# A two-layer hybrid mixer block in fp32 on one core: loads and residual sums of the downward MLP issued step by step, and the second layer's modulation computed in its own input projection

## The chip, the cores and the metric

The kernel runs on one core of one Trainium2 chip. The metric is the device time of one execution in microseconds, as the median of several runs. All data is fp32; a product is made of three matmuls of an fp32r high part and an fp32r rest (high x high, high x rest, rest x high).

## What is computed

Two layers (`DEPTH = 2`) over 1024 image tokens and 256 context tokens with 1024 channels. Each layer normalizes, modulates with a shift and a scale computed from a condition vector, projects into the columns of three mixers (an RWKV-7 scan, a gated delta net and a Fourier mixer), projects back, and ends with an MLP. Cut to what matters here:

```python
for l in range(DEPTH):
    last = l == DEPTH - 1
    m = (jax.nn.silu(c) @ w_mod[l] + b_mod[l]).reshape(b, N_MOD, 1, D_MODEL)
    mc = (jax.nn.silu(c_ctx) @ w_mod[l] + b_mod[l]).reshape(N_MOD, D_MODEL)
    uc = modulate(rmsnorm(xc, norm1_g[l]), mc[0], mc[1]) @ w_in[l]
    ux = modulate(rmsnorm(xl, norm1_g[l]), m[:, 0], m[:, 1]) @ w_in[l]
    ...                                   # the three mixers give yx (and yc)
    xl = xl + m[:, 2] * (yx @ w_out[l])
    hx = modulate(rmsnorm(xl, norm2_g[l]), m[:, 3], m[:, 4])
    xl = xl + m[:, 5] * sq_relu_mlp(hx, mlp_w1[l], mlp_w2[l])
    if not last:
        ...                               # the same for the context xc, with mc
return rmsnorm(xl, final_g)
```

The context is not carried behind the second layer, so that layer needs the modulation of columns 16 to 47 (in blocks of 128; shift and scale of the second norm, and the gates) for the image alone, one vector, where the first layer needs two.

## The kernel before, in words

`layer(l)` runs input projection, mixers and MLP one after the other; `run` calls it twice and then `final`. Tokens stand in pieces: A and B are 512 image tokens each, C is the context. In program order the stages are:

- **Input projection** (`layer`, from L2238). RWKV columns, gates z, Fourier columns, then 12 jobs of the delta net's convolution: a projection on PE, on DVE four multiply-adds and a scaling over up to 1282 columns (`gy`, `gu`), norms, and transposes on PE. Weights are 128 x 1024 blocks that `wsplit` (L281) loads as two raw tiles, copies to the high part on ACT and subtracts to the rest on POOL. The generator `mod` (L2242) is advanced at fixed places (L2249, L2250, L2269, L2270).
- **Modulation** (`mod_part`, L444). Twelve groups of four column blocks are made of eight loads of 256 KB each (tile `wmod`). The first of the eight is scaled on ACT into `macc`, each further one is a multiply-add on DVE (L462); for a second vector ACT scales and POOL adds (L464, L465). PE sums over the partitions (L474). In the first layer all groups from 16 on are made in the input projection; the second layer's twelve groups are made in the first layer's MLP (L1947).
- **Mixers** (`mixers`, L2034), whose end makes the output projections, the norms and the start of the MLP. From L2195 on it splits the weights of `early` blocks ahead.
- **MLP up** (`up`, L1613). One step of Strassen's scheme (Winograd's form) for the halves A and B of the tokens: 16 pairs of blocks with seven products of 12 matmuls each (`prod`, L1682), whose factors for the tokens are the tiles T1 to T4 and B22 (`norm_sums`, L559) and for the weights the tiles uS and uA (`up_parts`, L1567). While the sums for B are not ready, `ahead(n)` (L1642) makes the first `early` pairs' upper-left block from two plain products; such a pair later skips A11 and A12 and reads the result back (L1729). The squared activations and their sums go to DRAM as `h`.
- **Context down** (`context_down`, L1779, first layer only): 32 parts of 24 matmuls with 256 columns. Its caller (L1956) advances it and, from part 9 on, the first part of the downward pass.
- **MLP down** (`halves_down`, L1826): two halves f of the hidden blocks, seven products p in the order of `DOWN` (L39), eight steps n each. A step splits one `h` tile (loaded as `hraw`, five steps ahead) into `hu` on ACT and DVE (L1854, L1855) and one weight tile into `wu` on ACT and POOL (L1857, L1858), forms the next sums of weights in place on DVE (`we`, `wo`, `ws`; L1860 to L1866), and makes 12 matmuls (L1917). `ready(i + 2)` (L1909) is called two steps ahead of the matmuls. At n = 7 the four banks are drained on DVE and the residual `xrA` or `xrB` takes up finished sums (`add`, L1904; L1932 to L1940). The residual is brought back from DRAM by `back_x` (L1512), called at L1964 ahead of all steps; the odd weight tiles are loaded at L1888 to L1891.
- Behind the steps, `mlp` (L1946) makes the squares and sums for the next norm (L1983 to L2001).

Two things set the order of the work around the change. Every engine executes its queue in order, and all loads and stores go through the queue of SP in the order in which they were put there. The framework's scheduler orders independent instructions by the order of the program and by its own estimate of when operands are ready; a tile's place in memory is handed out in program order (`slot`, L163), and who gets it next waits for who had it. The kinds of places are x, w, u and h for tiles and r for raw ones (12 in the MLP, 6 in the input projection).

Of the kernel before, what the change touches and what calls it, by code (L numbers as in the profile page):

```python
# [35 lines left out]
DEC = 0.3032653298563167  # L36

HALVES = ("B11", "B21", "T2", "T3", "T4", "T1", "B22")
DOWN = ("A11", "A12", "S2", "S3", "A22", "S1", "S4")  # L39

COLS = (
# [68 lines left out]
class Net:  # L110
# [1502 lines left out]
    def up(self, l, last, mod, end):  # L1613
# [54 lines left out]
        ahead(1)  # L1668
        sums = self.norm_sums(l, self.kept)
        for n in range(2, 6):  # L1670
            next(sums)
            if n < self.early:
                ahead(n)
        for _ in chain(sums, self.pair):
# [151 lines left out]
    def halves_down(self, l, last):  # L1826
# [18 lines left out]
        def ready(i):  # L1845

            if i >= len(steps):
                return
            f, p, n = steps[i]
            fetch_h(i + 5)  # L1850
            w = {"A11": (even, 0), "A12": (odd, 0), "S2": (even, 0), "S3": (even, 1), "A22": (odd, 1), "S4": (odd, 0)}
            src = sums[n // 2][:, n % 2] if DOWN[p] == "S1" else w[DOWN[p]][0][n][:, w[DOWN[p]][1]]
            u, h, raw = us[i % 3], hs[i % 3], raws.pop(i)
            self.act(h[:, 0], raw)  # L1854
            V.tensor_tensor(h[:, 1], raw, h[:, 0].bitcast(F32), SUB)  # L1855
            self.free(raw)
            self.act(u[:, 0], src)  # L1857
            self.P.tensor_tensor(u[:, 1], src, u[:, 0].bitcast(F32), SUB)  # L1858
            e, o, s1 = even[n], odd[n], sums[n // 2][:, n % 2]
            if p == 0:  # L1860
                V.tensor_tensor(s1, e[:, 1], o[:, 1], ADD)
            elif p == 1:
                V.tensor_tensor(e[:, 0], s1, e[:, 0], SUB)  # L1863
            elif p == 2:
                V.tensor_tensor(e[:, 1], o[:, 1], e[:, 0], SUB)
                V.tensor_tensor(o[:, 0], o[:, 0], e[:, 0], SUB)  # L1866
            for q, ts, o in ((3, even, 0), (6, odd, 1)):
                if p == q:
                    if f == 0:
                        fetch(ts[n], 2 * (n + 8) + o)  # L1870
                    else:
                        self.free(ts[n])
            if p == 5 and f == 1 and n % 2:
                self.free(sums[n // 2])
# [10 lines left out]
                for j in range(5):  # L1885
                    fetch_h(j)
        yield
        for i in range(8):  # L1888
            yield from wait("u")
            odd.append(take("wo", "u"))  # L1890
            fetch(odd[i], 2 * i + 1)  # L1891
        while self.upward:
            yield
        yield "turn"
        for i in range(3):
            us.append(take("wu", "x", F32R))
            hs.append(take("hu", ("x", "x", "w!")[i], F32R))
# [2 lines left out]
        ready(1)  # L1900
        u2, u3 = [take("ms", "x") for _ in range(2)], []
        half = lambda t, b: t[b // 2][:, b % 2]

        def add(pc, b, t):  # L1904
            x = self.block(self.xr[pc], b)
# [2 lines left out]
        for i, (f, p, n) in enumerate(steps):  # L1908
# [6 lines left out]
            for b in range(4):  # L1915
                c = slice(b * 128, b * 128 + 128)
                self.mm3(ps[b], u[:, 0, c], u[:, 1, c], h[:, 0], h[:, 1], n == 0, n == 7)  # L1917
                if n == 7:
# [9 lines left out]
                    else:  # L1928
                        V.tensor_tensor(a, ps[b], a, ADD)  # L1929
                        if nm == "S1":  # L1930
                            V.tensor_tensor(z, ps[b], z, ADD)  # L1931
            for b in range(4) if n == 7 else ():  # L1932
                if nm == "A12":
                    add("A", b, half(u2, b))
                elif nm == "A22":
                    add("A", b + 4, half(u3, b))
                elif nm == "S1":
                    add("B", b + 4, half(u3, b))
                elif nm == "S4":
                    add("B", b, half(u2, b))  # L1940
            if f == 1 and n == 7 and p == 5:
                self.free(*u3)
            yield f, p, n
        self.free(*u2, *us, *hs)

    def mlp(self, l, last):  # L1946
        mod = iter(()) if last else self.mod_part(l + 1, 0, 48, True)  # L1947
        down = self.halves_down(l, last)
        self.upward = True
        if last:  # L1950
# [10 lines left out]
            self.gains(l + 1, 1)  # L1961
        while last and next(down) != "turn":
            pass
        for p in "AB":  # L1964
            self.back_x(f"xm{l}", p)
        sq, sc = [], []
        for f, p, n in down:
            if f == 0 and p == 0 and not last:
                if n == 0:
                    for j in range(2):  # L1970
                        self.squares("C", j, sc)
                elif n == 2:
                    self.rsum("C", sc)
                elif n == 4:
                    norm = self.norms(l + 1, 1, "C")
# [4 lines left out]
                    del self.xr["C"]  # L1980
            if f == 0:
                continue
            if (p, n) == (5, 0):  # L1983
                for j in range(4):
                    self.squares("A", j, sq)
            if (p, n) == (5, 3):
                self.rsum("A", sq)
                sq = []
            if (p, n) == (5, 7) and not last:
                self.first = [self.wsplit(self.win(l + 1, c), kind="w!") for c in (768, 256)]  # L1990
            if (p, n) == (6, 0):
                norm = iter(()) if last else self.norms(l + 1, 1, "A")
                for j in (2, 3):
                    self.squares("B", j, sq, "u")
            if p == 6:
                next(norm, None)
        for _ in norm:
# [36 lines left out]
    def mixers(self, l, last):  # L2034
# [159 lines left out]
        self.outproj(l, "B", yb, lambda b: b % 2 and self.squares("B", b // 2, self.sq))  # L2194
        self.at(1.6)  # L2195
        self.share = "uw"
        self.early = 4
        self.ahead = [self.wsplit(self.w1(l, 2 * n)) for n in range(self.early)]
        self.save_x(f"xm{l}", "B", False)
        self.raw = [self.up_load(l, fb) for fb in range(2)]  # L2200
# [10 lines left out]
    def layer(self, l):  # L2211
# [27 lines left out]
        self.set_rings(d=4, m=4)  # L2239
        self.rwkv_setup(l)  # L2240
        uk = self.rwkv_lora(l)
        mod = iter(()) if l else self.mod_part(l, 16, 48)  # L2242

        def others():

# [64 lines left out]
```

## Time and profile before

| | us |
|---|---|
| median of 3 runs | 4007.14 |
| lowest and highest | 3997.73 and 4032.35 |
| profiled execution, its own time | 4021.84 |
| its span, first to last instruction | 4020.1 |
| mean granted TensorE clock | 0.894 |

In the profiled execution the first layer's input projection runs from about 180 to 620 us, its mixers to 1290, its upward pass to 1776, the context's downward part until 1918 and its downward pass from 1880 to 2247 us. The second layer's input projection ends at about 2690 us, its mixers and output projections at 3325, its upward pass at 3664; its downward pass runs from 3657 to 3996 us, and `final` ends the span.

A line of the profile names engine, line of the kernel, instruction and tiles (written<-read). Most tiles are made by helpers, so that L257 is every matmul, L254 every ACT instruction and L264 every load; the tile tells them apart. A granted clock of 1.00 is TensorE at 2.4 GHz, 0.50 at 1.2 GHz; a value between is the mean of a stretch.

### The profile page before, as it was taken

Reading aid. Unit: us, or ns where it says so; the run is one execution under the profiler, and the core shown is the slowest. Engines: PE = TensorE matmul, PEld = TensorE weight load, DVE = VectorE, ACT = ScalarE, POOL = GpSimd, SP = SyncE. Lnnn points to the kernel's source line nnn. Section 1 sums busy time; section 2 is a strip of 40 time slices with the busy share of each in tenths; the row PEclk is TensorE's granted clock in tenths of the full one; section 3 lists DMA queues with packets and bytes.
Section 4 is the critical chain, followed back from the end, with each engine's and each line's share of the span. In section 5 each row is a group of like instructions: output and inputs, shape, how many; then the busy total and the mean of one; then the engine's idle time right before and its main releaser. Section 6 shows DMA issues by size and latency. Waiting matters only on the chain. (4 is left out here: it accounts for less than half of the span.)

```text
span 4020.1 us, 61983 instructions
## 1 busy us (share of the span) xinstructions
PE 3554.5 (88%) x23262; PEld 2971.3 (74%) x23262; DVE 2776.1 (69%) x4224; ACT 1619.5 (40%) x2947; POOL 1546.8 (38%) x1110
## 2 busy tenths in 40 slices
PE   8998996886888899998999989987698898998998
PEld 5776885775767788888778766876687776887777
DVE  5645777888764776566687744657878667767677
ACT  5433443333344444343434433433343344343443
POOL 1422435332225466434445322114333144554443
PEclk8999887877888999999999999997777898999999
DMA  6333436543466254578643232345344463447432
GB/s 219 107 127 139 122 113 177 150 147 94 132 178 199 88 168 142 169 243 284 194 127 115 67 134 102 105 119 176 98 140 128 149 193 106 158 154 256 157 110 82
DMA packets 546127, 589.83 MB, mean 147 GB/s; under 512 B 37654, under 2 KB 399650, under 8 KB 545826
## 3 DMA queue, kind: packets, MB, share of 16 engines
q1 hardware_dynamic: 545826, 585.86, 46.0%
q8 instruction: 183, 3.00, 0.3%
q14 instruction: 118, 0.97, 0.1%
HBM read 419.62 MB, written 166.10 MB: 146 GB/s over the span
## 5 line engine op out<-in xcount | busy, mean ns | idle before, releaser
L257 PE MATMUL bank<-hu,wu 128*128 128x512 f32 x2688 | 635.6, 398 | 32.5 <-DVE hu L1855 23.7
L294 POOL TENSOR_TENSOR wlo<-wraw,whi 128x512 fp32r<-128x512 f32 x264 | 356.7, 1372 | 777.3 <-ACT whi L254 413.5
L257 PEld LDWEIGHTS bank<-hu,wu 128*128 128x128 f32 x2688 | 514.1, 192 | 151.5 <-DVE hu L1855 32.9
L1855 DVE TENSOR_TENSOR hu<-hraw,hu 128x512 fp32r<-128x512 f32 x224 | 260.5, 1171 | 126.7 <-ACT hu L254 126.6
L1578 POOL TENSOR_TENSOR uS<-us,uS 128x512 fp32r<-128x512 f32 x128 | 193.8, 1528 | 168.7 <-ACT uS L254 155.8
L254 ACT ACTIVATE whi<-wraw 128x512 fp32r<-128x512 f32 (+1 forms) x296 | 178.8, 625 | 196.9 <-DMA wraw<-in_mlp_w_dram 53.0
L465 POOL TENSOR_TENSOR macc<-macc,wmod 128x512 f32<-128x512 f32 x84 | 135.6, 1615 | 188.2 <-ACT wmod L254 185.2
L254 ACT ACTIVATE ms<-ms 128x512 f32<-128x512 f32 x176 | 110.3, 627 | 241.1 <-DVE ms L1631 239.1
L257 PE MATMUL bank<-xhA,whi 128*128 128x512 f32 (+1 forms) x480 | 203.4, 425 | 0.0
L257 PE MATMUL bank<-xlA,whi 128*128 128x512 f32 (+1 forms) x480 | 199.8, 417 | 0.0
L257 PE MATMUL bank<-xhA,wlo 128*128 128x512 f32 (+1 forms) x480 | 197.8, 413 | 0.3 <-POOL wlo L294 0.3
L1858 POOL TENSOR_TENSOR wu<-we,wu 128x512 fp32r<-128x512 f32 x96 | 135.6, 1413 | 161.0 <-ACT wu L254 160.8
L462 DVE SCALAR_TENSOR_TENSOR macc<-wmod,cs,macc 128x512 f32<-128x512 f32 x140 | 135.2, 966 | 85.3 <-DMA wmod<-in_w_mod_dram 43.7
L1858 POOL TENSOR_TENSOR wu<-wo,wu 128x512 fp32r<-128x512 f32 x96 | 131.8, 1374 | 148.3 <-ACT wu L254 146.8
L1578 POOL TENSOR_TENSOR uA<-wraw,uA 128x512 fp32r<-128x512 f32 x96 | 142.5, 1491 | 98.2 <-ACT uA L254 85.8
L712 DVE SCALAR_TENSOR_TENSOR gy<-gu,vt,gy 128x1282 f32<-128x1282 f32 (+1 forms) x96 | 154.6, 1611 | 26.7 <-ACT gy L254 26.0
L1631 DVE TENSOR_TENSOR ms<-bank,ms 128x512 f32<-128x512 f32 x216 | 143.7, 683 | 38.6 <-PE bank L257 20.0
L257 PE MATMUL bank<-xhB,whi 128*128 128x512 f32 (+1 forms) x416 | 165.2, 397 | 5.0 <-ACT ru L254 5.0
L257 PE MATMUL bank<-xlB,whi 128*128 128x512 f32 (+1 forms) x416 | 164.7, 396 | 0.0
L257 PE MATMUL bank<-xhB,wlo 128*128 128x512 f32 (+1 forms) x416 | 164.0, 394 | 0.0
L845 DVE TENSOR_TENSOR iD<-iF,iE 128x31 f32<-128x31 f32 (+15 forms) x310 | 149.7, 484 | 6.5
L846 DVE TENSOR_TENSOR iE<-iE,iD 128x31 f32<-128x31 f32 (+15 forms) x310 | 144.2, 466 | 6.5
(525 smaller groups left out, 9719.6 us busy)
## 6 DMA issues: line engine op xcount, KB each, us to landing
hraw<-h SPq DMA_DIRECT2D x224, 256.0 KB
h<-ms SPq DMA_DIRECT2D x214, 256.0 KB
wraw<-in_mlp_w_dram SPq DMA_DIRECT2D x208, 256.0 KB
wmod<-in_w_mod_dram SPq DMA_DIRECT2D x192, 256.0 KB
wraw<-in_w_in_dram SPq DMA_DIRECT2D x100, 256.0 KB
wraw<-in_w_out_dram SPq DMA_DIRECT2D x80, 256.0 KB
we<-in_mlp_w_dram SPq DMA_DIRECT2D x32, 512.0 KB
wo<-in_mlp_w_dram SPq DMA_DIRECT2D x32, 512.0 KB
```

The costliest lines, as they stand in the source:

```text
L254: return self.S.activation(out, in_, func, **kw)
L257: return self.nc.tensor.matmul(out, lhsT, rhs, start=start, stop=stop)
L294: (self.V if even and i else self.P).tensor_tensor(lo[:, o + i:o + i + m], raw, h.bitcast(F32), SUB)
L462: V.scalar_tensor_tensor(acc[:, 0], raw, c[0], acc[:, 0], MUL, ADD)
L465: P.tensor_tensor(acc[:, 1], acc[:, 1], raw, ADD)
L712: V.scalar_tensor_tensor(y[:, a:b], u[:, a + t:b + t], w(t), y[:, a:b], MUL, ADD)
L845: V.tensor_tensor(t, F[:, m:, j:m].to_broadcast([128, n, m]), E[:, j:m, :m].to_broadcast([128, n, m]), MUL)
L846: V.tensor_tensor(E[:, m:, :m], E[:, m:, :m], t, SUB)
L1578: self.P.tensor_tensor(t[:, 1], w, t[:, 0].bitcast(F32), SUB)
L1631: V.tensor_tensor(out, ps, s, ADD)
L1855: V.tensor_tensor(h[:, 1], raw, h[:, 0].bitcast(F32), SUB)
L1858: self.P.tensor_tensor(u[:, 1], src, u[:, 0].bitcast(F32), SUB)
```

## The change

- In `halves_down` the eight odd weight tiles are taken behind the "turn"; two are loaded there and six in the steps of the first product, one per step.
- The three sums of weights move: `s1` from product 0 to product 1, the last difference from product 2 to product 3.
- A finished sum is no longer added to the residual at n = 7 but put in a list, from which each later step with n < 7 takes one. `u3` is freed later, and the squares and the sum of piece A, and the first squares of B, move by three or four steps.
- `back_x` is called behind the steps n = 7 of products 0 and 1 instead of ahead of all steps.
- `mod_part` in the first layer's MLP makes four groups instead of twelve; the second layer's input projection makes the other eight, as the first layer's does.
- `early` is 6 instead of 4 in the second layer.

```diff
+OUT = {"A12": (0, "A", 0), "A22": (1, "A", 4), "S1": (1, "B", 4), "S4": (0, "B", 0)}
@@ up
         for n in range(2, 6):
-            next(sums)
+            next(sums, None)
@@ halves_down, ready(i)
-            if p == 0:
+            if p == 0 and f == 0 and n < 6:
+                fetch(odd[n + 2], 2 * n + 5)
+            if p == 1:
                 V.tensor_tensor(s1, e[:, 1], o[:, 1], ADD)
-            elif p == 1:
                 V.tensor_tensor(e[:, 0], s1, e[:, 0], SUB)
             elif p == 2:
                 V.tensor_tensor(e[:, 1], o[:, 1], e[:, 0], SUB)
+            elif p == 3:
                 V.tensor_tensor(o[:, 0], o[:, 0], e[:, 0], SUB)
@@ halves_down
         yield
-        for i in range(8):
-            yield from wait("u")
-            odd.append(take("wo", "u"))
-            fetch(odd[i], 2 * i + 1)
         while self.upward:
             yield
         yield "turn"
+        odd += [take("wo", "u") for _ in range(8)]
+        for i in range(2):
+            fetch(odd[i], 2 * i + 1)
@@ halves_down, behind the matmuls of a step
-            for b in range(4) if n == 7 else ():
-                if nm == "A12":
-                    add("A", b, half(u2, b))
-                elif nm == "A22":
-                    add("A", b + 4, half(u3, b))
-                elif nm == "S1":
-                    add("B", b + 4, half(u3, b))
-                elif nm == "S4":
-                    add("B", b, half(u2, b))
-            if f == 1 and n == 7 and p == 5:
+            if n == 7 and nm in OUT:
+                t, pc, o = OUT[nm]
+                rest += [(pc, b + o, half(u3 if t else u2, b)) for b in range(4)]
+            if rest and (n < 7 or i == len(steps) - 1):
+                add(*rest.pop(0))
+            if (f, p, n) == (1, 6, 4):
                 self.free(*u3)
             yield f, p, n
+        for r in rest:
+            add(*r)
@@ mlp
-        mod = iter(()) if last else self.mod_part(l + 1, 0, 48, True)
+        mod = iter(()) if last else self.mod_part(l + 1, 0, 16, True)
-        for p in "AB":
-            self.back_x(f"xm{l}", p)
         for f, p, n in down:
+            if f == 0 and (p, n) in ((0, 7), (1, 7)):
+                self.back_x(f"xm{l}", "AB"[p])
-            if (p, n) == (5, 0):
+            if (p, n) == (5, 4):
                 for j in range(4):
                     self.squares("A", j, sq)
-            if (p, n) == (5, 3):
+            if (p, n) == (5, 6):
                 self.rsum("A", sq)
+            if (p, n) == (6, 4):
+                for j in (2, 3):
+                    self.squares("B", j, sq, "u")
             if (p, n) == (6, 0):
                 norm = iter(()) if last else self.norms(l + 1, 1, "A")
-                for j in (2, 3):
-                    self.squares("B", j, sq, "u")
@@ mixers
-        self.early = 4
+        self.early = 6 if last else 4
@@ layer
-        mod = iter(()) if l else self.mod_part(l, 16, 48)
+        mod = self.mod_part(l, 16, 48)
```

## Rows read from the trace of the kernel before

**Rows 1.** The page, part 1: busy time, share of the span, instructions.

```profile
PE 3554.5 (88%) x23262; PEld 2971.3 (74%) x23262; DVE 2776.1 (69%) x4224; ACT 1619.5 (40%) x2947; POOL 1546.8 (38%) x1110
```

**Rows 2.** Stretches: length, busy PE, PEld, DVE, ACT, POOL; clock, DMA share, GB/s.

```profile
180.00:376.00 196.00, 170.70 (x904) 134.71 (x903) 101.48 (x141) 64.44 (x120) 65.33 (x42) 0.93 0.38 133
376.00:600.00 224.00, 212.36 (x1081) 183.09 (x1080) 165.93 (x267) 100.45 (x156) 84.47 (x55) 0.85 0.40 123
1600.00:1750.00 150.00, 149.31 (x806) 129.28 (x806) 88.74 (x121) 65.02 (x125) 68.89 (x50) 1.00 0.50 166
1770.00:1880.00 110.00, 95.43 (x723) 93.62 (x723) 67.07 (x89) 43.31 (x71) 39.51 (x28) 0.91 0.91 304
1880.00:1940.00 60.00, 43.71 (x226) 36.60 (x225) 44.43 (x68) 21.14 (x39) 21.16 (x16) 0.86 0.69 243
2280.00:2500.00 220.00, 202.66 (x1006) 156.32 (x1005) 104.39 (x157) 75.38 (x138) 60.97 (x44) 0.95 0.33 111
2500.00:2690.00 190.00, 183.37 (x997) 156.02 (x996) 122.83 (x234) 74.16 (x117) 31.26 (x22) 0.96 0.29 95
3350.00:3377.00 27.00, 11.39 (x24) 6.11 (x23) 25.38 (x36) 14.44 (x25) 8.87 (x5) 0.56 0.33 100
```

**Rows 3.** Stretches of eight downward steps, work on hu alone, columns likewise.

```profile
1960.90:1983.40 22.50, 22.06 (x97) 17.94 (x96) 9.52 (x8) 4.93 (x8) 1.00 0.38 117
2005.20:2026.90 21.70, 21.70 (x97) 18.00 (x96) 10.20 (x8) 4.92 (x8) 1.00 0.33 97
2049.40:2075.50 26.10, 23.64 (x97) 19.11 (x96) 6.63 (x7) 4.92 (x8) 0.93 0.68 223
2075.50:2103.20 27.70, 24.12 (x98) 18.92 (x97) 9.35 (x8) 4.92 (x8) 0.94 0.24 66
2191.00:2219.50 28.50, 24.02 (x97) 18.75 (x96) 6.39 (x8) 4.92 (x8) 0.95 0.34 102
2219.50:2246.80 27.30, 24.35 (x97) 18.99 (x95) 6.24 (x6) 3.75 (x6) 0.93 0.12 39
3657.00:3696.90 39.90, 29.02 (x97) 21.49 (x98) 7.94 (x8) 4.36 (x7) 0.83 0.84 297
3807.10:3833.30 26.20, 23.73 (x98) 19.09 (x97) 7.33 (x7) 4.92 (x8) 0.93 0.68 226
3833.30:3859.30 26.00, 23.39 (x97) 18.89 (x96) 9.04 (x8) 4.93 (x8) 0.93 0.25 71
3947.30:3971.70 24.40, 22.42 (x98) 17.90 (x97) 8.23 (x8) 4.93 (x8) 1.00 0.12 33
```

**Rows 4.** DMA issues between 1745 and 1885 us: count, KB each.

```profile
wmod<-in_w_mod_dram SPq DMA_DIRECT2D x48, 256.0 KB
```

**Rows 5.** Waits of PE, 1770 to 1940 us: total us, times, longest.

```profile
PE bank L257 <- ACT whi L254: 11.9, 4, 6.2
PE bank L261 <- DVE rst L279: 4.1, 1, 4.1
```

**Rows 6.** Timeline of the DMA queue at the second layer's turn.

```profile
3672.59 6.51 SPq L264 DMA_DIRECT2D xrB<-xm  x8
3679.49 39.33 SPq L264 DMA_DIRECT2D hraw<-h  x25
```

**Rows 7.** Timeline of DVE after a product: start, length, instruction, count.

```profile
2053.40 4.34 DVE L1906 SCALAR_TENSOR_TENSOR xrB<-ms,mod,xrB 128x512 f32<-128x512 f32 x4
2057.67 1.88 DVE L1855 TENSOR_TENSOR hu<-hraw,hu 128x512 fp32r<-128x512 f32 x3
```

**Rows 8.** Waits of PE, 3345 to 3380 us.

```profile
PE bank L257 <- ACT T2h L254: 9.8, 3, 8.2
```

**Rows 9.** Tile macc, whole span: duration min/median/max in ns.

```profile
L462 DVE SCALAR_TENSOR_TENSOR macc<-wmod,cs,macc x140: 735/752/1857, 126.7 to 1885.3; 128x512 f32<-128x512 f32 x140
```

**Rows 10.** Timeline of PE: one group of modulation columns summed.

```profile
1865.99 1.05 PE L257 MATMUL bank<-cst,macc 128*128 128x1 f32 x8 [0.79 <-DVE macc L462]
```

**Rows 11.** Waits of PE, 376 to 600 us.

```profile
PE bank L261 <- DVE gr L751: 7.9, 3, 2.8
```

More of the change, by code (lines that the diff above doesn't have):

```diff
@@ L1902, in halves_down @@
         half = lambda t, b: t[b // 2][:, b % 2]
+        rest = []
         def add(pc, b, t):
```

## The prediction

> **What bounds the kernel now.** I read the page first: PE is busy for 88% of the span and no other engine for over 74% [rows 1]. So the time is PE's own work plus the places where PE stands or runs at the lower of its two clocks (1.2 instead of 2.4 GHz; the granted clock of 1.00 in the rows is the higher one). The change takes no product away, so it can only be worth what is lost in those places. I therefore cut the span into stages and read for each the length, PE's busy time and the granted clock [rows 2, 3]. The loss of a stretch is at most (length minus PE busy) plus (1 minus clock) times length; it is a little less, since idle time at the low clock is counted twice.
>
> A downward product is 8 steps of 12 matmuls. Undisturbed, its 96 matmuls take 21.7 us, 0.226 us each, as in the stretch from 2005.2 us [rows 3]. Against this measure the reader sees in the same group where the downward pass loses: 18.2 us at the second layer's turn from up to down (39.9 us in place of 21.7), 4.3 to 6.0 us in each product that follows an S1 or S4 product in the first half (26.1, 27.7, 26.2, 26.0), 0.8 us after an A12 (22.5), and 6.8 and 5.6 us in the last two products of the first layer. The late upward stretch, 1600 to 1750 us, loses 0.7 us [rows 2]; there is nothing to win there. The context's downward part and the first layer's turn, 1770 to 1940 us, lose 14.6 + 9.9 and 16.3 + 8.4, together 49 us, with the DMA engines at a share of 0.91 and 304 GB/s in the first of the two stretches [rows 2]. The start of the second layer's upward pass, 3350 to 3377 us, has 24 matmuls where 27 us would hold 119: 27 - 24 x 0.226 = 21.6 us lost [rows 2].
>
> **The change part by part.** All terms are against the profiled execution, 4021.84 us.
>
> *Modulation out of the first layer's MLP.* Eight of twelve groups leave, 64 loads of 256 KB. Between 1745 and 1885 us alone the queue issued 48 of them [rows 4], 12.6 MB; at 304 GB/s that is 41 us of transfer in a stretch of 140 us whose weights PE waits for (ACT's split of whi, 11.9 us in 4 waits) [rows 5]. Together with *the odd weights and the residual behind the turn* (12 transfers of 0.25 to 0.5 MB no longer ahead of hraw) this empties the queue when the context's last weights and the first hraw need it. What stays of the 49 us: the first wait of 6.2 us, which ends with the upward pass's own last activations; the context's norm between the two stages, 4.1 us for its rst [rows 5] and about 3 for its squares; and the low clock that follows such gaps, about 6. So 19 stay and 30 go. Ends: 12, if only the loads behind the turn help, and 42.
>
> *The second layer's turn.* The queue issues xrB as 8 pieces over 6.5 us, and hraw only at 3679.5 us [rows 6], after which the product runs on. Moving the residual to steps 7 and 15 removes that. What is late next is the end of the upward pass on DVE, some 5 us of the 18.2. The new order asks for one hraw and one odd tile per step in product 0, 0.79 MB in 2.71 us = 290 GB/s, about what the turn moves now (297) [rows 3], so it is just covered by the five hraw fetched ahead, 5 x 2.71 = 13.6 us; uncovered, 4 us would come back. The residual's first half is 2 MB, 7 us at that rate, with 8 steps until its first use. I take -12; ends -16 and -6.
>
> *Residual sums put off.* After S1, DVE has 8 sums out of PSUM and then 4 residual sums of 4.34 us in one run; the hu of the third step starts behind them, at 2057.67 us [rows 7], and PE stands. One sum in each of the next four steps is not in front of anything. DVE then has in product 0 hu and one sum, in product 1 hu and the two weight sums (s1 moves there), in product 2 hu, one weight sum and one residual sum: at most three per step, as in product 2 now, whose 22.5 us hold 0.8 of loss from A12's sums [rows 3]. Removed: 4.4 + 6.0 + 4.5 + 4.3 for the four large ones and 6 x 0.8 for the small ones (products 2 and 5 of the first half and 2 of the second, in both layers), 24.0, of which I leave 2: -22. Ends -26 and -12. In the last two products (rows from 2191.0, 2219.5 and 3947.3) squares and the sum of A move 3 to 4 steps later, closer to S1's sums and to the norm that needs them, so what the residual sums free is spent again: -1, ends -6 and +6.
>
> *Six pairs ahead.* PE's wait from 3350 us is for T2h (9.8 us, longest 8.2) [rows 8], which ACT and DVE make; DVE is busy for 25.4 of these 27 us [rows 2]. Two more pairs are 2 x 24 matmuls x 0.226 = 10.9 us that PE does there instead of later. Their weights are split on POOL, which is busy for 8.9 of the 27 us and done with the other four by then. Two more sums on DVE delay T2 by about 2. I take -9; ends -15 (the higher clock is kept) and -4 (the halves of T wait for slots that the two pairs hold).
>
> *Modulation into the second layer's input projection.* 64 loads, 8 ACT, 56 multiply-adds on DVE with a median of 0.752 us [rows 9], 42 us, and 8 groups of PE work of 1.05 us [rows 10]; the last only moves. The trace has no such projection of one column, but it has the first layer's, with two columns: 196 + 224 us, loss 25.3 + 13.7 and 11.6 + 33.6. The second layer's, without modulation, loses 17.3 + 11.0 and 6.6 + 7.6 in 220 + 190 us [rows 2]. The difference is 11 and 31, 42 us, mostly low clock; part of it are three waits for gr, 7.9 us, on DVE [rows 11]. Two columns have twice the PE and nine times the ACT work (72 instructions against 8), and 56 sums on POOL that one column has not. I take +17, a little under half; ends +3 (DVE's 42 us fit into its idle time of 115.6 + 67.2 us) and +42. DVE executes in order, so a multiply-add whose wmod is late holds the convolution's sums behind it, and PE for these; the transfers have room (DMA share 0.29 to 0.33). SP's queue gets 64 loads between the weights' loads; they wait for one of six raw slots that the multiply-adds free, which held no weight back in the first layer.
>
> Sum: -30 - 12 - 22 - 1 - 9 + 17 = -57 us, so 3964.8 in the profiled execution. That one stands 0.37% above the median of the runs shown (4007.14); the same share off gives a predicted median of 3950.
>
> **The rivals.**
> *The moved modulation costs as much as two columns did* (+42) and the context stage keeps its pace for other reasons than transfers (-12): -12 - 12 - 22 - 1 - 9 + 42 = -14, 3993. For it: the half-clock stretches of the first layer's projection begin at its DVE waits. Against: POOL's sums and eight ninths of the ACT work fall away.
>
> *Slower: DVE's queue becomes the bound of the second layer's projection.* If each of the 56 multiply-adds is held by a POOL instruction, it takes the 1.857 us of the slowest one [rows 9], 104 us, and if none of it falls into idle time the sum is -74 + 104 = +30, 4037. It decides from 74 / 56 = 1.3 us per multiply-add on PE's path. Against it: the median is 0.752, and DVE idles for 183 us in these stretches [rows 2]. The Trainium skill, page "SBUF — State Buffer", section "Who interferes with whom", says that a DVE instruction with two SBUF inputs and a GpSimd one that reads SBUF exclude each other for a whole instruction, which is a rule against putting 56 such instructions beside the weights' splits. The trace agrees for single ones (maximum beside median), not for the bulk.
>
> *More goes than I count*: context -42, turn -16, sums -26, pairs -15, last products -6, projection +3: -102, 3905. For it: each low-clock stretch that a removed wait started goes too.
>
> *The turn doesn't change*, since the same bytes are asked for in the same 40 us at a DMA share of 0.84 [rows 3]: 12 and about 15 us come back, -30, 3977. I count it in the first rival's chance.
>
> **How the numbers follow.** A measurement of this kernel tells about 1% from no change, that is 3967 to 4047. Forecast 0.62, its own range 3922 to 3978; first rival with the unchanged turn 0.19; slower one 0.07; more than counted 0.12. Faster by over 1%: 0.85 of the forecast's 0.62, all of the last 0.12, and 0.04 of the first rival: 0.69. Slower by over 1%: half of 0.07, 0.04. Within 1%: the rest, 0.27. The range from 3900 to 3995 takes in both neighbours and leaves out the slower case.
>
> **What would show it.** Right: no wmod issue after about 1650 us, and the stage from 1770 us over some 30 us earlier; the second layer's product 0 in under 30 us; four products now at 26 to 28 us at 22; about 72 matmuls in the 27 us after the fourth pair; macc instructions between 2300 and 2660 us with a median near 0.75 us and the clock there above 0.90. Wrong: a clock under 0.88 or new waits for gr and gu in the second layer's projection, hu waiting for hraw in product 0 or for DVE in products 1 and 2, and a last product of the first layer that waits longer for rst.

## The result, and the profile after

Median after 3965.76 us (4 runs, 3962.36 to 3968.44) against 4005.68 us before in the same rounds (4 runs): ratio 0.9883, 95% interval 0.9859 to 0.9907, so 1.2% faster. The forecast was 3950, the range 3900 to 3995. The profiled span is 3964.7 us, 55.4 less than before; the sum of the terms was -57. By the medians the change is worth 39.9 us: before's profiled execution stood 14.7 us above the median of its first three runs, after's (3966.45) only 0.7 above its own. So the sum was nearly right for the two profiled executions alone, and its terms were not. Cut at the first or last matmul of each stage (the second projection at VectorE's last convolution sum), the two traces give (us):

| stage | before | after | difference | forecast |
|---|---|---|---|---|
| first layer, up to the context's first product | 1771.4 | 1769.2 | -2.2 | 0 |
| context and first turn, to product 1 | 167.8 | 122.2 | -45.6 | -30 |
| product 1 to the end, first layer | 307.6 | 301.1 | -6.5 | -23 in |
| product 1 to the end, second layer | 299.5 | 292.6 | -6.9 | both layers |
| second projection, to its last convolution | 459.4 | 479.1 | +19.7 | +17 |
| mixers and output projection | 619.5 | 612.1 | -7.4 | 0 |
| six pairs: from there to the first downward product | 331.4 | 331.5 | +0.1 | -9 |
| second layer's product 0 | 39.8 | 32.8 | -7.0 | -12 |
| `final` | 23.7 | 24.1 | +0.4 | 0 |

The stages that the sum priced give -46.2; the other -9.2 come from stages for which it had 0, the mixers above all.

The page's first part, beside [rows 1]:

```profile
PE 3529.3 (89%) x23262; PEld 2950.1 (74%) x23262; DVE 2789.9 (70%) x4224; ACT 1624.3 (41%) x2947; POOL 1550.1 (39%) x1110
```

The same stretches as in [rows 2], in after's time (length, busy PE, PEld, DVE, ACT, POOL; clock, DMA share, GB/s): context, first product of the first layer, second projection, and the 27 us after the fourth pair.

```profile
1769.20:1867.10 97.90, 95.33 (x771) 94.83 (x770) 55.98 (x59) 43.08 (x70) 46.68 (x32) 0.97 0.92 310
1867.10:1891.40 24.30, 24.10 (x117) 19.91 (x116) 22.80 (x40) 11.48 (x22) 9.23 (x8) 1.00 0.63 203
2192.50:2671.60 479.10, 439.67 (x2282) 358.35 (x2282) 308.45 (x501) 179.19 (x300) 111.65 (x76) 0.94 0.44 139
...
3307.60:3334.60 27.00, 17.79 (x73) 13.72 (x72) 25.12 (x37) 18.04 (x31) 4.22 (x3) 0.85 0.29 91
```

PE waits between 1769 and 1892 us, beside [rows 5]:

```profile
PE bank L258 <- ACT whi L255: 1.9, 1, 1.9
PE bank L258 <- POOL wlo L295: 0.7, 1, 0.7
PE bank L262 <- DVE rst L280: 0.2, 1, 0.2
```

The context loses 2.6 us of busy time and 0.03 of the clock where [rows 2] showed 14.6 and 0.09. The DMA share is still 0.92: the queue is as full as before, but no wmod [rows 4] is issued between 1745 and 1885 us any more. The waits of 11.9 us for whi and 4.1 for rst are down to 1.9 and 0.2. The six groups' own products in that stage, 48 small matmuls, are gone too.

Stretches of eight downward steps, work on hu alone, beside [rows 3]: first layer's product 0 of the second half, the one behind it, the last one; then the second layer's product 0 and product 0 of its second half.

```profile
2025.90:2053.20 27.30, 23.47 (x98) 17.55 (x96) 7.89 (x8) 4.93 (x8) 1.00 0.26 73
2053.20:2075.10 21.90, 21.90 (x97) 17.94 (x96) 11.26 (x10) 4.93 (x8) 1.00 0.38 108
...
2164.10:2192.50 28.40, 25.09 (x97) 18.62 (x95) 7.12 (x7) 3.69 (x6) 0.94 0.11 38
3615.20:3648.00 32.80, 26.19 (x96) 19.89 (x96) 7.12 (x8) 4.32 (x7) 0.90 0.84 298
...
3779.90:3807.20 27.30, 23.39 (x98) 17.53 (x96) 7.90 (x8) 4.92 (x8) 1.00 0.27 74
```

The products that should have come down from 26 to 28 us to 22 did so only in part: the two behind S1 (product 6 of the first half) take about 23, the two behind S4 still 27.2 and 27.3. By product, both layers together: the four large losses shrank by 5.3 us (forecast 19.2), the six small ones behind A12 by 4.4 (4.8), the last two products of each layer by 6.6 (1), and product 1 of the first layer, which was at 21.8, takes 24.4 (as it does with the modulation moved alone). The timeline of VectorE in the first product behind S4 (start, length, instruction, count) shows what stands there now, beside [rows 7]:

```profile
2030.31 0.67 DVE L1856 TENSOR_TENSOR hu<-hraw,hu 128x512 fp32r<-128x512 f32 x1
2030.91 3.11 DVE L1910 SCALAR_TENSOR_TENSOR xrB<-ms,mod,xrB 128x512 f32<-128x512 f32 x3
2033.94 1.77 DVE L1856 TENSOR_TENSOR hu<-hraw,hu 128x512 fp32r<-128x512 f32 x1
2035.64 0.74 DVE L1910 SCALAR_TENSOR_TENSOR xrB<-ms,mod,xrB 128x512 f32<-128x512 f32 x1
2036.30 2.98 DVE L1865 TENSOR_TENSOR we<-ws,we 128x512 f32<-128x512 f32 x3
2039.20 1.75 DVE L1856 TENSOR_TENSOR hu<-hraw,hu 128x512 fp32r<-128x512 f32 x1
2040.87 0.68 DVE L1865 TENSOR_TENSOR we<-ws,we 128x512 f32<-128x512 f32 x1
```

"One sum in each of the next steps" holds in the program, not in VectorE's queue. The scheduler put three residual sums together, and then three sums of weights that belong to product 1, several steps early, in front of the hu of the next step. PE waits 2.2 us for that hu.

### The profile page after: what moved, and what is told of

Read it like the earlier page. It is cut to its first block, busy times and chain, and to the rows that moved or that the text cites. A ratio compares the mean times of both kernels' runs of the same rounds, so it can differ in the third digit from the quotient of the medians.

```text
span 3964.7 us, 62054 instructions
## 1 busy us (share of the span) xinstructions
PE 3529.3 (89%) x23262; PEld 2950.1 (74%) x23262; DVE 2789.9 (70%) x4224; ACT 1624.3 (41%) x2947; POOL 1550.1 (39%) x1110
## 5 line engine op out<-in xcount | busy, mean ns | idle before, releaser
L295 POOL TENSOR_TENSOR wlo<-wraw,whi 128x512 fp32r<-128x512 f32 x268 | 366.5, 1388 | 753.9 <-ACT whi L255 538.3
L258 PE MATMUL bank<-hu,wu 128*128 128x512 f32 x2688 | 625.1, 393 | 20.5 <-DVE hu L1856 12.1
L258 PEld LDWEIGHTS bank<-hu,wu 128*128 128x128 f32 x2688 | 504.9, 189 | 138.3 <-DVE hu L1856 21.0
L1579 POOL TENSOR_TENSOR uS<-us,uS 128x512 fp32r<-128x512 f32 x128 | 184.7, 1456 | 177.6 <-ACT uS L255 166.8
L258 PE MATMUL bank<-xhA,whi 128*128 128x512 f32 (+1 forms) x496 | 211.8, 428 | 6.0 <-ACT whi L255 5.1
L258 PE MATMUL bank<-xlA,whi 128*128 128x512 f32 (+1 forms) x496 | 207.9, 420 | 0.1
L258 PE MATMUL bank<-xhA,wlo 128*128 128x512 f32 (+1 forms) x496 | 206.2, 417 | 1.2 <-POOL wlo L295 1.2
```

What stands on the lines that cost most here:

```text
L258: return self.nc.tensor.matmul(out, lhsT, rhs, start=start, stop=stop)
L295: (self.V if even and i else self.P).tensor_tensor(lo[:, o + i:o + i + m], raw, h.bitcast(F32), SUB)
L1579: self.P.tensor_tensor(t[:, 1], w, t[:, 0].bitcast(F32), SUB)
```

## The experiments

Unless it says otherwise a kernel is the one after with one edit, seen in one profile. The same stage of the same code moves by itself: see the kernel after again, below, before reading the mixers.

**Four pairs instead of six.**

```diff
-        self.early = 6 if last else 4
+        self.early = 4
```

> The changed kernel with early = 4 in the second layer too. In the changed kernel the stretch from the second layer's last output projection to the end of its upward pass has the same length as before (331.7 against 331.5 us), though the wait at its start lost 15.7 instead of 22.8 us; some ten small waits of 0.4 to 1.6 us on DVE's sums (ms) appeared behind it. Theory A, the small waits belong to other parts of the change: they stay, the start loses 7 to 9 us more, the span is 3972 to 3974 us. Theory B, the six pairs brought them: they go, the start loses 7 to 9 more, the span stays within 3 us of 3964.7.

From the last output projection to the first downward product 331.3 us, against 331.5: theory B, the two pairs are worth nothing. PE does 72 matmuls in the 27 us behind the fourth pair, as forecast, and is about 7 us ahead there. It gives that back later; 4.7 us of it show as small waits, which this kernel does not have. Waits of PE in the rest of the upward pass, first after, then with four pairs:

```profile
PE bank L258 <- DVE ms L1632: 5.9, 11, 1.6
```

```profile
PE bank L258 <- DVE ms L1632: 1.2, 2, 0.7
```

The reason stands in VectorE's waits of the two kernels: a sum of weights that waits for its transfer, with the drain of a bank queued behind it. After, that is the second sum of a pair (11 waits, 40.8 us); with four pairs it is the first (11 waits, 45.2 us), which stands at a place where PE is not yet short of a bank. That the place makes the difference was read from the two timelines, not tried.

**All of the second layer's modulation back in the MLP.**

```diff
-        mod = iter(()) if last else self.mod_part(l + 1, 0, 16, True)
+        mod = iter(()) if last else self.mod_part(l + 1, 0, 48, True)
-        mod = self.mod_part(l, 16, 48)
+        mod = iter(()) if l else self.mod_part(l, 16, 48)
```

> The changed kernel with all twelve modulation groups of the second layer back in the first layer's MLP. In the changed kernel the stretch from the context's first downward matmul to the first layer's downward product 1 takes 122.2 us (before: 167.8). Theory A, the modulation's loads made that stretch long: it takes 145 to 165 us, the second layer's projection gets about 20 us shorter, and the span is 3970 to 3985 us. Theory B, the loads behind the turn did it: the stretch stays under 135 us, and the kernel is faster than the changed one by the 10 to 20 us of the projection (span 3945 to 3957).

Theory A: context and turn 156.1 us instead of 122.2, the second projection 465.3 instead of 479.1, the span 20.1 more.

**The modulation's move alone, on the kernel before.** The same two lines the other way.

> The kernel before with only the modulation's eight last groups moved to the second layer's projection; odd weights, residuals, sums and pairs stay as they were. From the context's first product to the second product of the first layer's downward turn it was 167.8 us before, 122.2 after, and 156.1 with all but the modulation changed. Theory A (each part takes its own share, they add): 167.8 - 34 = 134, 130 to 139. Theory B (the modulation's loads are the whole of it, the odd weights only look good): 120 to 128. Theory C (either part alone leaves the queue full, and both are needed): over 145. From the end of the first downward turn to the last convolution of the second layer's projection: 475 to 482, as after, where 459.4 was before.

The stage takes 120.3 us: theory B, and less than with the whole change. Its row (columns as above) and the same of the experiment before it:

```profile
1763.10:1883.40 120.30, 118.25 (x885) 113.62 (x884) 79.69 (x98) 54.22 (x92) 56.82 (x40) 0.99 0.87 293
```

```profile
1766.50:1922.60 156.10, 135.97 (x932) 128.16 (x931) 104.98 (x149) 61.10 (x100) 56.39 (x40) 0.91 0.84 286
```

Both move about the same bytes per second at the same share; one has 42 wmod loads in between, and PE idles 20 us. ScalarE's waits for the weights' transfers in the stage (total, times, longest) before, with the modulation moved alone, and with it back in the MLP:

```profile
ACT whi L254 <- DMA wraw<-in_mlp_w_dram: 50.6, 27, 15.1
ACT whi L254 <- DMA wraw<-in_mlp_w_dram: 19.1, 29, 4.3
ACT whi L255 <- DMA wraw<-in_mlp_w_dram: 53.5, 32, 17.2
```

So the weights come late when the modulation is there. No run keeps the modulation's 40 multiply-adds on VectorE and leaves out its loads, so the share of each is not shown: the queue itself waits there for places that the multiply-adds free, 11.9 us before and 14.8 with the modulation back. The two parts do not add: with the modulation in the MLP, all the rest of the change was worth 167.8 - 156.1 = 11.7 us here; without it, nothing. This edit alone takes 45.0 us off the span of before's profile (3975.1; one run, 33.8 us below the median of before in its rounds). The second projection grows by 15.1 us (474.5), and the second layer's product 0 stays at 40.5.

**Residual sums all at once again.**

```diff
-                rest += [(pc, b + o, half(u3 if t else u2, b)) for b in range(4)]
-            if rest and (n < 7 or i == len(steps) - 1):
-                add(*rest.pop(0))
+                for b in range(4):
+                    add(pc, b + o, half(u3 if t else u2, b))
```

> The changed kernel with the four residual sums of a product added at once at n = 7, everything else as changed. From downward product 1 to the end of the downward pass the changed kernel takes 301.1 us (layer 1) and 292.6 us (layer 2), before 307.6 and 299.5; undisturbed it would be 283. Theory A (the forecast's size, 22 us for both layers): the two get longer by 10 to 12 us each, to 311 and 303, longer than before. Theory B, the weight sums that the scheduler puts into the same places take half of what the residual sums freed: 5 to 7 us longer each, about as before.

Theory B: from product 1 to the end 306.4 and 298.7 us against 301.1 and 292.6. The sums put off are worth 5.3 + 6.1 = 11.4 us, half of the forecast. They do not lie where it put them: 4.4 us in the six small losses and 4.9 in the last two products of each layer, but only 2.2 in the four large ones. There the two products behind S1 are 4.5 us shorter with the sums put off and the two behind S4 2.3 us longer.

**Residual ahead of the steps again.**

```diff
+        for p in "AB":
+            self.back_x(f"xm{l}", p)
-            if f == 0 and (p, n) in ((0, 7), (1, 7)):
-                self.back_x(f"xm{l}", "AB"[p])
```

> The changed kernel with the residual of A and B brought back ahead of all downward steps, as before. The second layer's product 0 takes 32.8 us as changed, 39.8 before. Theory A, the residual's transfers ahead of hraw made it late: 38 to 42 us again, and 8 to 12 us more in the first layer's context stretch as well, span 3980. Theory B, the odd weights did it: under 35 us, span within 4 us of 3964.7.

In the first layer the stage up to product 1 takes 130.9 us instead of 122.2: with the odd weights loaded behind the turn, the residual seems to stand in their way. With both as before (the modulation alone) it was 120.3, so the two moves together bring nothing there. In the second layer the loss only changes its place. Products 0 and 1 (columns as above):

```profile
3617.70:3646.50 28.80, 24.87 (x97) 18.72 (x96) 24.38 (x30) 11.96 (x22) 12.12 (x8) 0.94 0.95 362
3646.50:3673.00 26.50, 23.57 (x98) 17.58 (x97) 26.02 (x31) 9.83 (x18) 14.06 (x8) 1.00 0.44 136
```

Together 55.3 us, against 32.8 + 21.8 = 54.6 after. PE waits there for hu on VectorE, 6.1 us in 8 waits. So the order of transfers is not what holds the second layer's turn any more.

**Each sum of weights held behind the hu of its own step,** and four pairs. The dependence orders VectorE's queue alone; no semaphore is added.

```diff
-            V.tensor_tensor(h[:, 1], raw, h[:, 0].bitcast(F32), SUB)
+            hu = V.tensor_tensor(h[:, 1], raw, h[:, 0].bitcast(F32), SUB)
...
-                V.tensor_tensor(s1, e[:, 1], o[:, 1], ADD)
+                behind(V.tensor_tensor(s1, e[:, 1], o[:, 1], ADD), hu)
...
+        info = mybir.DependencyInfo(mybir.DependencyClass.NoSync, mybir.DependencyReason.DATA)
...
+        def behind(i, h):
+            self.tc.add_manual_dep(getattr(i, "ins", i), getattr(h, "ins", h).name, info, reason="behind")
```

> The kernel after with four pairs instead of six, and with each sum over weights held behind the hu of its own step on VectorE, where it had run ahead in twos and threes. Theory A (these runs ahead are what is left of the losses in the downward products): from product 1 to the end 301.1 becomes 289 to 294 in the first layer and 292.6 becomes 285 to 288 in the second, 12 to 17 us together; the span falls to 3948 to 3954 and the time to about 3952. Theory B (VectorE has the same work in all, and what is put later delays another step): no product part changes by over 3 us, and the time stays at 3960 to 3968.

Neither theory. From product 1 to the end nothing is won (301.5 and 293.4): the loss in front of product 1 is gone (1.4 + 2.5 + 1.1 us in steps 0, 4 and 6 of product 0 of the second half, now 0), but the sums of product 2 now stand in front of the drains of product 1, 2.1 us at its first step. The gain is where it was not looked for: the second layer's product 0 falls from 32.8 to 24.2 us (with four pairs alone it took 33.0). VectorE there, first after, then in this kernel:

```profile
3626.17 0.68 DVE L1864 TENSOR_TENSOR ws<-we,wo 128x512 f32<-128x512 f32 x1
...
3627.38 0.68 DVE L1864 TENSOR_TENSOR ws<-we,wo 128x512 f32<-128x512 f32 x1
3627.98 0.68 DVE L1856 TENSOR_TENSOR hu<-hraw,hu 128x512 fp32r<-128x512 f32 x1
3629.82 1.77 DVE L1865 TENSOR_TENSOR we<-ws,we 128x512 f32<-128x512 f32 x1 [1.16 <-POOL wu L1859]
3631.51 3.46 DVE L1867 TENSOR_TENSOR we<-wo,we 128x512 f32<-128x512 f32 x2
3634.89 0.68 DVE L1856 TENSOR_TENSOR hu<-hraw,hu 128x512 fp32r<-128x512 f32 x1
```

```profile
3606.59 3.04 DVE L1856 TENSOR_TENSOR hu<-hraw,hu 128x512 fp32r<-128x512 f32 x2 [0.35 <-ACT hu L255]
3611.01 0.69 DVE L1856 TENSOR_TENSOR hu<-hraw,hu 128x512 fp32r<-128x512 f32 x1 [1.37 <-ACT hu L255]
3612.05 1.36 DVE L1856 TENSOR_TENSOR hu<-hraw,hu 128x512 fp32r<-128x512 f32 x1 [0.35 <-ACT hu L255]
```

After, VectorE stands 1.16 us for a wu that a sum of weights needs done, makes three such sums in 5.2 us, and only then the next hu, 6.2 us after the one before was done. With the sums held, nothing but ScalarE's half of hu is in front of it. Median 3954.86 us (4 runs, 3940.41 to 3964.65), ratio to before 0.9863, 0.9831 to 0.9896; this interval overlaps after's.

**Without the eight groups.** A constant of 0.5 stands for their columns, with no loads, sums or products.

```diff
-        mod = self.mod_part(l, 16, 48)
+        mod = iter(()) if l else self.mod_part(l, 16, 48)
+        if l:
+            self.V.memset(self.lv[l]["m"][:, 16:48], 0.5)
```

> The kernel after without the modulation's eight last groups of the second layer: a constant of 0.5 stands in their place, with no load, no sum and no product. It prices the modulation in the projection by itself. Theory A (the modulation is the whole of the 19.7 us that the projection grew by): from the end of the first downward turn to the last convolution 479.1 becomes 458 to 463, and to the last output projection 1091.2 becomes 1076 to 1081. Theory B (part of the growth comes from where the scheduler puts the rest, and the modulation is mostly hidden): 468 to 479, and 1085 to 1091.

The second projection takes 461.2 us: theory A, 17.9 us for the eight groups (that the whole to the output projection's end came out at 1063.8, below the expectation, lies in the mixers, which vary). PE waits 25.8 us in this stage, 31.8 after, and the groups' own products take 0.81 us each, 6.5 in all; the other 5 or so are spread thinly and were not traced to a place. One pair of profiles is not sharp here: over the profiles of this study the projection takes 459.4 to 465.4 us without the eight groups and 474.5 to 481.4 with them on VectorE, some 15 us apart in the mean.

**Multiplied on ScalarE and added on GpSimd,** on the kernel with the sums held.

```diff
+                elif n == 1:
+                    self.act(raw, raw, AF.Identity, scale=c[0])
+                    P.tensor_tensor(acc[:, 0], acc[:, 0], raw, ADD)
```

> The kernel of the sums held behind hu, and besides the eight groups in the second layer's projection multiplied on ScalarE and added on GpSimd (as the second column of the other groups is), where VectorE did both in one instruction. Theory A (what the modulation costs there is its place in VectorE's queue, 56 instructions of 0.83 us): the projection falls from 479.1 to 462 to 469, and the time is 8 to 15 us below the one without it. Theory B (GpSimd's sums beside VectorE's, or ScalarE's queue, cost as much): 475 to 485 or more, and no gain.

Theory B, and more: the projection takes 511.9 us, the time is 3984.39 (6 runs), 29.5 above the kernel without it. Groups of instructions in the projection, first after, then here (busy us, mean ns | idle before):

```profile
L713 DVE SCALAR_TENSOR_TENSOR gy<-gu,vt,gy 128x1282 f32<-128x1282 f32 (+1 forms) x48 | 74.1, 1544 | 8.1 <-ACT gy L255 7.8
...
L463 DVE SCALAR_TENSOR_TENSOR macc<-wmod,cs,macc 128x512 f32<-128x512 f32 x56 | 46.6, 833 | 28.6 <-ACT macc L255 20.2 <-DMA wmod<-in_w_mod_dram 8.1
```

```profile
L464 POOL TENSOR_TENSOR macc<-macc,wmod 128x512 f32<-128x512 f32 x56 | 98.5, 1761 | 119.7 <-ACT macc L255 73.3 <-ACT wmod L255 25.6 <-DMA fwf<-in_fn_w_dram 18.0
L716 DVE SCALAR_TENSOR_TENSOR gy<-gu,vt,gy 128x1282 f32<-128x1282 f32 (+1 forms) x48 | 83.9, 1747 | 10.5 <-ACT gy L255 10.1
```

46.6 us on VectorE become 98.5 on GpSimd and 39.0 on ScalarE, and VectorE's convolution sums take 9.8 us longer beside them. PE's waits rise from 31.8 to 51.8 us; 7.1 of the 51.8 are one wait for a whi, 4.1 one for macc itself. The convolution's sums that meet no GpSimd instruction in time take at most 1.56 us in either kernel; of those that meet one, 15 after and 23 here, the mean is 1.71 and 2.12.

**The sums of products 2 and 3 three steps later,** past the drains and the residual sums, on the kernel with the sums held; and **the kernel after again** in the same rounds.

```diff
-            elif p == 2:
-                behind(V.tensor_tensor(e[:, 1], o[:, 1], e[:, 0], SUB), hu)
+            m = (n - 3) % 8
+            if (2, 3) <= (p, n) < (3, 3):
+                behind(V.tensor_tensor(even[m][:, 1], odd[m][:, 1], even[m][:, 0], SUB), hu)
...
```

> The kernel of the sums held behind hu, and the sums of the third and fourth product three steps later, past the four drains and the four put-off residual sums that they had stood in front of. Theory A (the 2.1 to 2.9 us that the third product newly lost, twice per layer, are VectorE's order alone): step 0 of both third products at 0 to 0.5, from product 1 to the end 301.5 becomes 295 to 298 and 293.4 becomes 287 to 290, the span 8 to 11 us under the one without it in the same stages, the time some 12 to 20 us below after's in the same runs. Theory B (GpSimd beside VectorE sets it, whatever the order): the loss moves to the steps at n of 3 to 5, and nothing is won.

> The kernel after, unchanged, on the same chip and in the same rounds as the kernel of the sums put three steps later, so that the two can be compared: 3960 to 3970 if the state of the chip makes no difference. Its stages beside after's first profile show how far one stage moves without any edit: I expect under 2 us for the downward products and up to 8 us for the mixers of either layer.

3947.50 us (5 runs, 3946.29 to 3956.72), ratio to before 0.9847, 0.9823 to 0.9871; after again 3962.88 (6 runs, 3951.91 to 3975.70), 0.9881, 0.9856 to 0.9905. By the medians 15.4 us, or 0.4%, in favour of the new order; the two intervals overlap a little. The stages agree: product 0 of the second layer 23.4 us (after again 33.0), from product 1 to the end 300.5 and 289.8 (301.2 and 292.6), so the first layer does not reach the 295 to 298 of theory A. The step behind the drains still loses 1.4 us, not the 0 to 0.5 of theory A. The new order's product 0 in the second layer (columns as above):

```profile
3611.60:3635.00 23.40, 22.31 (x97) 17.93 (x96) 16.44 (x19) 11.71 (x21) 11.18 (x8) 1.00 0.97 356
```

After again also shows what a stage does by itself: the downward products agree with after's first profile within 0.2 us, the second projection takes 481.4 us against 479.1, the mixers and output projection of the second layer take 616.8 us against 612.1. Over all profiles of this study that stage lies between 602.6 and 619.5, whatever was edited. So the -7.4 us in the table is no effect of the change that could be shown.

**The eight groups in the first layer's upward pass,** on the kernel of the sums three steps later: all of them, with four advances of the generator per pair, and four of them, with three.

```diff
             u4 = total(tile(), prod("S1", "T1"), u2)
             done("S1")
+            next(mod, None)
...
-        mod = iter(()) if last else self.mod_part(l + 1, 0, 16, True)
+        mod = iter(()) if last else self.mod_part(l + 1, 0, 48, True)
```

> The kernel with the sums put three steps later, and all twelve groups of the second layer's modulation in the first layer's upward pass, which now advances them four times per pair instead of twice; none in the context's downward part and none in the projection. From the first T2 to the context's first product it was 407.5 us after (408 in the kernel before that has two groups more there). Theory A (the upward pass has room on VectorE, 89 of 150 us busy, and on the queue, so only the eight groups' own products of 0.81 us are paid): 411 to 417 there, the projection 459 to 463 instead of 479, the context and the turn unchanged at 120 to 123, the time 9 to 15 us below the kernel with the sums three steps later, about 3936. Theory B (in the upward pass the multiply-adds stand in front of the drains of the banks, as the sums did in the downward pass): 422 or more there, and nothing won.

> The same with three advances per pair: eight groups in the first layer's upward pass and four in the second layer's projection. Theory A: 409 to 412 in the upward pass, the projection 468 to 472, the time 4 to 8 us below the kernel with the sums three steps later. Theory B: 415 or more, and nothing won.

By the numbers theory B in both, by another mechanism: 446.7 and 422.1 us in the upward pass, where the kernel without the move took 409.9. Waits of PE there with all groups moved:

```profile
PE bank L258 <- DVE macc L463: 20.8, 5, 9.8
PE bank L258 <- POOL macc L466: 9.8, 3, 5.3
```

No drain is among them. A group's eight small products stand in PE's own queue right behind its last multiply-add, and PE waits for them with the pass queued behind. That is not all of the 36.8 us: PE's waits of every kind grew from 24.8 to 41.1 us, the products themselves take 6.5, and the rest goes with a granted clock of 0.91 in place of 0.96. The projection fell to 463.7 us with all groups gone, but with four left it took 479.8, as long as with eight (475.9); why is open. Times 3977.84 (6 runs) and 3956.78 (4 runs), ratios to before 0.9915 and 0.9856 (0.9832 to 0.9880): by the median the kernel without the move remains the fastest, but from the one with four groups moved it can't be told apart.

## Why the prediction was right, and where it was not

The time lay in the range and the sum was 1.6 us off, by luck: terms that were too large made up for one that was too small, and 9.2 us came from stages that it had at nothing. Against the medians the sum was 17 us too large. Most of the gap from 3950 to 3965.76 is one step, that after's profiled execution would stand as far above its median as before's: 14.8 us were taken off for that, and it stood 0.7 above.

- *Context and first turn,* -30 against -45.6, outside its bounds of -42 to -12. The step that failed is "19 stay": I left the first wait of 6.2 us to the upward pass's last activations, 7 to the context's norm and 6 to the clock. Those waits went with the modulation, as the run with it alone shows (47.5 us); that they were the full queue is argued from ScalarE's waits for weights. Of the 45.6, 4.9 are the six groups' own products (0.81 us each), which the term did not hold; without them 40.7 of the 49 went and about 8 stayed in place of 19. The 41 us of transfer that I had worked out for the loads was the better estimate of what goes.
- *Second projection,* +17 against +19.7, of which the eight groups are 17.9 by the run without them and some 15 over all profiles. The size held, the step less so: 6.5 us of it are the groups' own products, which "only moves" left out, so the loads and multiply-adds cost about 9 to 11 and not 17. That it stays well under two columns' 42 because POOL's sums are absent is what the run on GpSimd shows from the other side. What was feared as "mostly low clock" did not come: 0.94 in place of 0.95 or 0.96.
- *Residual sums and last products,* -23 against -13.4. The direction was right (11.4 us are lost again when the sums are made at once), and the small losses went as forecast. The step that failed is "One sum in each of the next four steps is not in front of anything", and with it "at most three per step": both counted the program's order. The queue has the weights' sums in runs of three ahead of the hu, 5 us in product 0 of the second half in either layer, so that the four large losses gave 5.3 us in place of 19.2. The last products gave 6.6 in place of 1, which hid part of that.
- *Second layer's turn,* -12 against -7.0. The transfers were no longer the bound; what I took to be late next (VectorE) was late by more, 8.7 us of it the same sums of weights, ahead of their step. Beside that the residual's place, on which the forecast built, was worth 0.7 us over products 0 and 1. With the sums held and put later the turn loses under 2 us, at 356 GB/s, above the 290 that I set against the 297 of [rows 3] as nearly the limit.
- *Six pairs,* -9 against 0. The 72 matmuls came; what failed is the silent step that a lead at the start is kept. It was gone by the end of the pass, most of it, as the timelines read, in eleven waits behind a late transfer.

Of the rivals, none came: the projection did not cost 42, and of the slower case only the pieces show. In the second projection the 56 multiply-adds have a median of 0.746 us, a few up to 1.781, and a mean of 0.833, far from the 1.3 us per multiply-add from which it decides. Moved to GpSimd they take 1.761 us each and slow VectorE's own sums by 13%. The rule of the Trainium skill that the prediction weighed ("SBUF — State Buffer", section "Who interferes with whom") speaks of just this pairing. The traces agree: the 45 multiply-adds on VectorE that meet no GpSimd instruction in time take at most 0.753 us, the 11 that meet one up to 1.781, and with the sums on GpSimd 23 of the 48 convolution's sums meet one, in place of 15.

## What to carry to other kernels

When a stretch with a full DMA queue loses time in several places (weights, a norm, the clock), price the removal of the foreign work at the greater part of that loss, as here (40.7 of 49 us): the small waits there need not have causes of their own. Count the products that move with the work in both stages. An order written as "one per step" is a fact of the program only; read the engine's queue in the timeline, and tie an instruction to the one that it must not overtake. A lead gained at one place is only worth what the next stage, in steady state, does not hand back.

## What the runs showed of the hardware

- The same VectorE instruction on 128 x 512 takes 0.68 us at some times and 1.75 to 1.79 us at others. In after's trace all 28 hu (of 224) that meet no GpSimd instruction in time take 0.675 to 0.691 us; of the 196 that meet one, 156 take over 0.9, up to 1.784. Three sums of weights in a row took 1.88 us in one kernel and 2.98 in another. A step's budget of 2.72 us holds three short ones, or one long and one short.
- With the transfers of the second layer's turn in front of it, the core moved 356 GB/s at a DMA share of 0.97 (sums three steps later) and 362 at 0.95 (residual ahead), where the kernel before had moved 297 at 0.84 [rows 3].
- In the context's stage, with its queue full, the modulation cost most of its loads' transfer time. Back in the MLP it had 42 loads there, 11.0 MB, 38 us at the stage's 286 GB/s; the stage was 33.9 us longer, 4.9 of it the products of six groups.
